# Latents scaled in the weight loop and turned ahead of the indexer; transposes over two kinds of PSUM banks; GpSimd's residual passes moved in the code

## The chip, the core and the metric

The kernel runs on one core of a Trainium2 chip. The core has TensorE (PE, matrix products; PEld is its weight load), VectorE (DVE), ScalarE (ACT) and GpSimd (POOL) for arithmetic, and SyncE (SP), whose queue issues nearly all loads here. Each engine works its own queue in order; the order within each queue is fixed when the kernel is built. The metric is the device time of one execution in microseconds (us), the median of several runs. The profile is of one execution of its own.

## The reference

All data is float32. `x` has 256 tokens of 1024 features. Block 1 (two layers of attention and MLP, with a context of 256 further tokens) comes first and is not changed by this diff but for the end of its last MLP. Block 2 has two layers, each of the form below (cut to what matters).

```python
h = x * (1 + scale) + shift                      # modulation, from a second conditioning vector
p_cq, p_ckv, p_kr, p_qb, ..., p_qi, p_ki, p_wi, p_gate = split(h @ w_in[l])
cq, ckv = rms_norm(p_cq, q_norm_g[l]), rms_norm(p_ckv, kv_norm_g[l])   # the latents: 768 and 256 features
qa, ka, va = heads(cq @ w_uq[l]), heads(ckv @ w_uk[l]), heads(ckv @ w_uv[l])
o_a = mla_attention(qa, rope part of qa, ka, rope(p_kr), va)
o_b = dilated_attention(qb, kb, vb)
score = sum_h w_idx[h] * relu(q_idx[h] . k_idx)  # the indexer
o_c = attention of each query over its top 64 keys by score
y = concat(o_a, o_b, o_c) * silu(p_gate)
x = layer_norm(4 ** 0.25 * x + (1 + gate) * (y @ w_out[l]), ln_g[l], ln_b[l])
```

The first layer's `x` is an RMS norm of block 1's result. So between block 1 and layer 0, and again between layer 0 and layer 1, the same thing has to happen: a norm over tokens, the modulation, and a transpose into feature-major form for the next products. A second copy of the normed `x`, times 4 ** 0.25 and without the modulation, is the residual that each layer's end needs.

## The kernel before

**Tiles.** The 256 tokens are two token tiles `t` of 128. Token-major tensors are [128 tokens, 1024 features]; the input of the products is feature-major, in two float32r parts, `hi` and `lo` (`ahi`, `alo`), each as two tiles of four 128-feature chunks. Every product is three matmuls (`mm3`, lines 317 to 322: hi x hi, lo x hi, hi x lo). Large tensors share one pool of 24 buffers (`k4`), small column vectors one pool of 48 (`sm`). PSUM's eight banks are four "mm", two "s", one "pt" and one "om".

**Weights.** `Weights` walks a fixed plan (class `Weights`, L169). SP loads a piece of 512 KB into one of four `raw` buffers (L184); ACT casts it to `whi` (L197); DVE subtracts to get `wlo` (L199), five buffers each, two pieces ahead of use. `W.hold` names a DVE instruction behind which all later `wlo` splits have to be issued.

**The order of the work.** The code is written as one long sequence; when the kernel is built, a planner lays each engine's queue in order from a model of durations, taking what is ready by its model, code order first.

**End of block 1 (`mlp1`).** For each token tile: the last products, gate and residual (L1227, L1228), sum of squares on ACT (L1229), the power -1/2 on POOL (L330, in `rsqrt`), then z = x * rstd * gr (L1235), z + sr (L1236), and `turn_input` for each half of the features: four transposes into the bank "pt" (L1248), `ahi` by ACT (L1250), `alo` by DVE (L1251). Each call for half 0 sets `W.hold`, so the later call, of token tile 1, is the one that the next layer's splits stand behind. Then POOL makes the residual in place, in two passes a token tile (L1239, L1240).

**`block2_layer`.** A loop over 14 weight pieces computes, for both token tiles, the two halves of the latents (key 0 and 1; L1563 multiplies by the gain row `lgain`, L1567 sums squares) and two value tensors (key 2 and 3), token tile 1 three pieces behind token tile 0. The gain's load waits, through a one-element copy on POOL (`after`, L358), for the residual of token tile 0 (`xa[0]`). Then come the indexer's inputs (`b2misc`, `b2qi`), the indexer (`sel`: per head a score step on DVE, then 16 rounds of the 8 largest and their removal, L1495 and L1496, each round with a new `sm` tile), and only then `latents(t)`: three small DVE steps, the power, the scales (L1589, L1590), four groups of transposes all in bank "pt" (L1594), copies by ACT and DVE (L1596, L1597) into `chi` and `clo`. After that the q and k products of the second attention (L1630 takes them out of PSUM), three pairs of its heads, the products from the latents, three pairs, the indexer's attention in two pairs, the gate and the output projection. `finish(t)` norms a token tile as it is done (L1737, L1740) and turns it. Behind both, with the order fixed by hand behind the second power and the last `ahi` copy, the residual for the next layer: a scaling of `lnb` (L1756), two small POOL steps a tile (L1760, L1761), ACT's scaling (L1763), and four POOL passes (L1766), tile 0 and 1 times `lng`, then tile 0 and 1 plus `lnb`.

Of the kernel before, what the change touches and what calls it, by code (L numbers as in the profile page):

```python
# [270 lines left out]
class Net:  # L271
# [897 lines left out]
    def mlp1(self, a):  # L1169
# [25 lines left out]
        for e in range(8):  # L1195
            hid[e] = [self.k4([128, 4, 256], F32R, name="hid") for _ in range(2)]
            for g in range(2):
                relu2(e, g, self.narrow("m1w1", a, "s").rearrange("p a b -> p (a b)"))
            if e == 0:

                xt = [self.k4([128, 1024], name="xt") for _ in range(2)]
                for k in range(0, 8, 4):
                    for t in range(2):
                        pt = self.psum("pt", [128, 4, 128])
                        for kk in range(4):
                            nc.tensor.transpose(pt[:, kk], hx[k + kk][:, cols(t)], self.ident)
# [12 lines left out]
        for t in range(2):  # L1219
            for i in (0, 2, 1, 3):  # L1220
                product(7, i, t, ws[i])
# [3 lines left out]
            for i in range(2):  # L1225
                c = cols(i, 512)
                V.tensor_tensor(z[:, c], acc[t][i], gate[:, c], op=OP.mult)  # L1227
                V.tensor_tensor(x[:, c], z[:, c], x[:, c], op=OP.add)  # L1228
                nc.scalar.activation(z[:, c], x[:, c], AF.Square, accum_out=ss[:, i:i + 1])  # L1229
            s1 = self.sm([128, 1])  # L1230
            V.tensor_tensor(s1, ss[:, 0:1], ss[:, 1:2], op=OP.add)
            rstd = self.rsqrt(s1, 1, 1.0 / D, 1e-6, True)
            for i in range(2):
                c = cols(i, 512)
                V.scalar_tensor_tensor(z[:, c], x[:, c], rstd, gr[:, c], op0=OP.mult, op1=OP.mult)  # L1235
                V.tensor_tensor(z[:, c], z[:, c], sr[:, c], op=OP.add)  # L1236
                self.turn_input(z[:, c], i, t, hi4, lo4)
            with self.tc.issue_after(self.pow.ins):
                nc.gpsimd.tensor_scalar(x, x, rstd, ALPHA, op0=OP.mult, op1=OP.mult)  # L1239
                nc.gpsimd.tensor_tensor(x, x, fr, op=OP.mult)  # L1240
        return [[t[:, i] for t in f for i in range(4)] for f in (hi4, lo4)], xt

    def turn_input(self, u, i, t, hi4, lo4):

        nc = self.nc
        pt = self.psum("pt", [128, 4, 128])
        for k in range(4):
            nc.tensor.transpose(pt[:, k], u[:, cols(k)], self.ident)  # L1248
        hv, lv = (f[i][:, :, cols(t)] for f in (hi4, lo4))
        self.last_hi = nc.scalar.copy(hv, pt)  # L1250
        op = nc.vector.tensor_tensor(lv, pt, hv.bitcast(F32), op=OP.subtract)  # L1251
        if i == 0:
            self.W.hold = op.ins


# [274 lines left out]
                                     start=kt == 0, stop=kt == qt)  # L1530
        nc.scalar.copy(yt, o)

    def block2_layer(self, l, a, xa):
# [13 lines left out]
        def token_step(i, t, w):  # L1547
# [13 lines left out]
            else:  # L1561
# [3 lines left out]
                for j in range(key + 1):  # L1565
                    cc = slice(256 * j, 256 * j + 512 // (key + 1))
                    nc.scalar.activation(junk[:, cc], ps[:, cc], AF.Square, accum_out=cst[t][:, key + j:key + j + 1])  # L1567

        steps = ([(g, 2 * i, 2, 512) for g in range(2) for i in range(4)] + [(2, 2 * i, 2, 384) for i in range(4)]
                 + [(3, 4 * i, 4, 256) for i in range(2)])  # L1570
        LAG, ws = 3, {}
        for i in range(len(steps) + LAG):
# [2 lines left out]
                token_step(i, 0, ws[i])  # L1575
            if i >= LAG:
                token_step(i - LAG, 1, ws.pop(i - LAG))
        chi4, clo4 = ([self.k4([128, 4, 256], F32R, name=n) for _ in range(2)] for n in ("chi", "clo"))
        chi, clo = ([t[:, i] for t in f for i in range(4)] for f in (chi4, clo4))

        def latents(t):

            s = cst[t]
            V.tensor_tensor(s[:, 0:1], s[:, 0:1], s[:, 1:2], op=OP.add)
            V.tensor_scalar(s[:, 0:1], s[:, 0:1], 256.0 / 768, None, op0=OP.mult)
            V.tensor_copy(s[:, 1:2], s[:, 2:3])
            r = self.rsqrt(s[:, 0:2], 2, 1.0 / 256, 1e-6, True)
            u = lat[t]
            V.tensor_scalar(u[:, 0:768], u[:, 0:768], r[:, 0:1], None, op0=OP.mult)  # L1589
            V.tensor_scalar(u[:, 768:1024], u[:, 768:1024], r[:, 1:2], None, op0=OP.mult)  # L1590
# [26 lines left out]
        for g in range(2):  # L1617
            nc.scalar.copy(qi[:, 2 * g:2 * g + 2], self.narrow("b2qi", a))
        sel = self.indexer(l, qi, ki, wi)
        for t in range(2):  # L1620
            latents(t)
        yt = self.feats(8, 256, name="yt")

        qb, kb = (self.k4([128, 3, 256], name="qkb") for _ in range(2))
# [127 lines left out]
                    finish(t)  # L1752
        if l == 1:
            return None, None

        nc.gpsimd.tensor_scalar(lnb, lnb, ALPHA, 0.0, op0=OP.mult, op1=OP.add)  # L1756
        for x, (mv, rstd) in zip(z, mvs):
            r2, nb = self.sm([128, 1]), self.sm([128, 1])
            with self.tc.issue_after(self.pow.ins):
                nc.gpsimd.tensor_scalar(r2, rstd, ALPHA, 0.0, op0=OP.mult, op1=OP.add)  # L1760
                nc.gpsimd.tensor_scalar(nb, mv[:, 0:1], r2, -1.0, op0=OP.mult, op1=OP.mult)  # L1761
            with self.tc.issue_after(self.last_hi.ins):
                nc.scalar.activation(x, x, AF.Identity, bias=nb, scale=r2)  # L1763
# [3 lines left out]
        return (hi, lo), z  # L1767

    def rope2(self, x, n):

# [17 lines left out]
def build(nc, tc, A, out, stop=9):  # L1788
    with tc.tile_pool(name="sb", bufs=1) as sb, tc.tile_pool(name="ps", bufs=1, space=PSUM) as ps:
# [2 lines left out]
        if stop <= 1:  # L1792
            return
        a = net.block1_l1(a)
        a, xa = net.mlp1(a)
        if stop <= 2:
            return
        for l in range(2):
            a, xa = net.block2_layer(l, a, xa)
            if stop <= 3 + l:  # L1800
                return

# [17 lines left out]
```

## Time and profile before

| What | us |
|---|---|
| Median of 3 runs (lowest to highest) | 1473.42 (1472.79 to 1475.20) |
| Profiled execution, its own time | 1476.02 |
| Its span | 1474.2 |
| PE busy | 1382.9 |
| DVE busy | 1016.8 |
| ACT busy | 639.2 |
| POOL busy | 270.7 |
| Handover 1 (end of `mlp1`, start of layer 0) | about 1027 to 1060 |
| Layer 0, latents' transposes | 1128 to 1137 |
| Handover 2 (end of layer 0, start of layer 1) | about 1249 to 1284 |
| Layer 1, latents' transposes | 1344 to 1352 |

Times in the profile count from the span's start. A timeline row shows a start, a duration, the engine, the line and the operation with what it writes and reads, how many instructions the row joins, and in brackets how long the engine was idle before it and what released it. A row that joins several instructions gives the time from the first one's start to the last one's end. In a window row each engine's busy time stands with its number of instructions; PEclk is the TensorE clock that was granted, as a share of 2.4 GHz. Busy PE is not PE at its peak, and the time between the span and the execution's own time (1.8 us) lies around the span.

### The profile page before, as it was taken

To read this page: it belongs to the slowest core of one execution; us is meant where nothing else is said; L and a number is where in the kernel's file an instruction comes from. 1 tells how busy PE (TensorE), PEld (TensorE's weight loads), DVE (VectorE), ACT (ScalarE), POOL (GpSimd) and SP (SyncE) were. 2 spreads that over 40 slices of the span, in tenths; PEclk is the share of its full clock that TensorE was granted. 3 is DMA by queue.
4 is the path that set the end of the run, shared out by engine and by line. 5 is a ranking of instruction groups with operands and counts; after the bars stand their busy time and mean duration, and the time that the engine had idled before them with its cause. 6 is when DMAs were issued, how large, how long until landed. Compare 5 with 4: busy or idle time off the path is not lost.

```text
span 1474.2 us, 23024 instructions
## 1 busy us (share of the span) xinstructions
PE 1382.9 (94%) x8779; PEld 1166.3 (79%) x8779; DVE 1016.8 (69%) x1879; ACT 639.2 (43%) x1221; POOL 270.7 (18%) x290
## 2 busy tenths in 40 slices
PE   6899999999999999999999999999796999796997
PEld 4776668988878777888989989898696788695786
DVE  4586666648977889878677664455657668666666
ACT  4355444342223222245565564444353554352552
POOL 0200011230011213441000131111200315400312
PEclk9999999999999999999999989999898999998999
DMA  9825551136578887833132266556272354473331
GB/s 320 271 72 189 172 190 40 58 115 203 177 247 272 271 300 261 275 106 118 59 100 72 86 207 204 182 179 200 81 209 85 119 192 146 132 198 105 125 123 71
DMA packets 183438, 240.79 MB, mean 163 GB/s; under 512 B 22399, under 2 KB 147360, under 8 KB 183328
## 3 DMA queue, kind: packets, MB, share of 16 engines
q1 hardware_dynamic: 172960, 235.37, 49.7%
q10 hardware_dynamic: 8576, 3.89, 1.0%
q8 instruction: 69, 1.13, 0.3%
q0 software_dynamic: 1792, 0.06, 0.1%
q14 instruction: 41, 0.34, 0.1%
HBM read 237.26 MB, written 2.03 MB: 162 GB/s over the span
## 4 chain that ended last, share of the span: by engine, by line
PE 74%; DVE 13%; DMA 4%; issue 3%; POOL 3%; ACT 2%; SPq 0%; ACTq 0%; DVEq 0%; POOLq 0%
PE mm L320 17%; PE mm L321 17%; PE mm L322 17%; PE s L321 3%; PE s L322 3%; PE s L320 3%; DVE wlo L199 2%; PE om L1074 2%; DMA adaw<-in_ada_w 2%; PE s L1512 1%; PE pt L1059 1%; PE om L1529 1%; PE mm L499 1%; PE om L1400 1%; ACT whi L197 1%
## 5 line engine op out<-in xcount | busy, mean ns | idle before, releaser
L199 DVE TENSOR_TENSOR wlo<-raw,whi 128x1024 fp32r<-128x1024 f32 (+3 forms) x282 | 355.9, 1268 | 186.3 <-ACT whi L197 176.8
L197 ACT CAST whi<-raw 128x1024 fp32r<-128x1024 f32 (+3 forms) x282 | 289.6, 1034 | 329.2 <-PE mm L321 175.9
L320 PE MATMUL mm<-ahi,whi 128*128 128x256 f32 (+1 forms) x848 | 288.1, 340 | 0.0
L321 PE MATMUL mm<-alo,whi 128*128 128x256 f32 (+1 forms) x848 | 285.0, 336 | 0.0
L322 PE MATMUL mm<-ahi,wlo 128*128 128x256 f32 (+1 forms) x848 | 284.8, 336 | 0.0
L320 PEld LDWEIGHTS mm<-ahi,whi 128*128 128x128 f32 x848 | 164.0, 193 | 20.4 <-issue 3.6
L322 PEld LDWEIGHTS mm<-ahi,wlo 128*128 128x128 f32 x848 | 163.3, 193 | 18.2 <-issue 2.4
L321 PEld LDWEIGHTS mm<-alo,whi 128*128 128x128 f32 x848 | 163.6, 193 | 16.0 <-issue 1.8
L366 POOL TENSOR_TENSOR hid<-e,hid 128x512 fp32r<-128x512 f32 x48 | 78.1, 1627 | 353.9 <-ACT hid L365 353.7
L531 DVE SCALAR_TENSOR_TENSOR acc<-adaw,cst,acc 128x1024 f32<-128x1024 f32 x98 | 128.0, 1320 | 0.5 <-DMA adaw<-in_w_ada 0.2
L320 PE MATMUL mm<-hid,whi 128*128 128x512 f32 (+1 forms) x288 | 106.7, 371 | 0.0
L321 PE MATMUL mm<-hid,whi 128*128 128x512 f32 (+1 forms) x288 | 106.0, 368 | 0.0
L322 PE MATMUL mm<-hid,wlo 128*128 128x512 f32 (+1 forms) x288 | 105.9, 368 | 0.0
L320 PE MATMUL s<-ahi,whi 128*128 128x256 f32 x256 | 73.1, 286 | 1.2 <-ACT ahi L367 1.2
L321 PE MATMUL s<-alo,whi 128*128 128x256 f32 x256 | 72.9, 286 | 0.1
L322 PE MATMUL s<-ahi,wlo 128*128 128x256 f32 x256 | 72.7, 284 | 0.0
L321 PE MATMUL mm<-wlo,ahi 128*128 128x256 f32 (+1 forms) x192 | 64.2, 335 | 6.5 <-DVE wlo L199 6.5
L320 PE MATMUL mm<-whi,ahi 128*128 128x256 f32 (+1 forms) x192 | 65.1, 340 | 2.8 <-ACT ahi L1250 2.8
L322 PE MATMUL mm<-whi,alo 128*128 128x256 f32 (+1 forms) x192 | 63.7, 333 | 0.0
L320 PEld LDWEIGHTS mm<-hid,whi 128*128 128x128 f32 x288 | 54.1, 188 | 10.2 <-issue 0.4
L322 PEld LDWEIGHTS mm<-hid,wlo 128*128 128x128 f32 x288 | 54.2, 188 | 9.7
L321 PEld LDWEIGHTS mm<-hid,whi 128*128 128x128 f32 x288 | 54.2, 188 | 9.2
(352 smaller groups left out, 2856.2 us busy)
## 6 DMA issues: line engine op xcount, KB each, us to landing
raw<-in_mlp_w SPq DMA_DIRECT2D x128, 512.0 KB, 4.2
adaw<-in_ada_w SPq DMA_DIRECT2D x96, 512.0 KB, 4.7
raw<-in_w_in SPq DMA_DIRECT2D x64, 512.0 KB, 4.0
adaw<-in_w_ada SPq DMA_DIRECT2D x48, 512.0 KB, 4.8
raw<-in_odd_w_in SPq DMA_DIRECT2D x24, 512.0 KB, 4.1
raw<-in_w_out SPq DMA_DIRECT2D x16, 512.0 KB, 5.4
raw<-in_even_w_in SPq DMA_DIRECT2D x12, 512.0 KB, 6.0
raw<-in_even_w_out SPq DMA_DIRECT2D x8, 512.0 KB, 3.5
```

The costliest lines, as they stand in the source:

```text
L197: self.nc.scalar.copy(hi[:, :m], raw)
L199: self.nc.vector.tensor_tensor(lo[:, :m], raw, hi[:, :m].bitcast(F32), op=OP.subtract)
L320: mm(ps, w[0], x[0], start=start, stop=False, skip_group_check=skip)
L321: mm(ps, w[0], x[1], start=False, stop=False, skip_group_check=skip)
L322: mm(ps, w[1], x[0], start=False, stop=stop, skip_group_check=skip)
L366: return (lo_eng or nc.vector).tensor_tensor(lo, t, hf, op=OP.subtract)
L499: nc.tensor.matmul(ps[32 * j:32 * j + 32], self.cs1[:, k, :], raw[:, 256 * j:256 * j + 256], start=k == 0, stop=k == 7)
L531: V.scalar_tensor_tensor(acc, raw, s, acc, op0=OP.mult, op1=OP.add)
L1059: nc.tensor.transpose(pt[:, kt], e[:, cols(kt)], self.ident)
L1074: nc.tensor.matmul(o[64 * hh:64 * hh + 64, cols(qt)], self.v[ab][:, 4 - nkt + i, cols(j // 2, 64)], PT[:, i, hh], start=i == 0, stop=i == ...
L1400: nc.tensor.matmul(o, PT[:, kt], self.vs[g][:, kt, cols(hh)], start=kt == 0, stop=kt == 3)
L1512: nc.tensor.matmul(s[:, c0:c0 + n], qf(h, cols(qt)), kf(h, slice(0, n)), start=True, stop=True)
```

## The change

- In `mlp1` the first transposes of `x` use the banks "pt" and "om" in turn, and `turn_input` uses "pt" for half 0 and "s" for half 1.
- In `mlp1` the squares go to a scratch tile; the product with the row `gr` is a pass of its own ahead of the power; behind it one pass does both the multiply by rstd and the add of `sr`.
- `W.hold` is set only by the first turned half of token tile 0.
- The residual is made by a function `resid(t)` that the next layer calls, in the code behind its latents; the hand-made order of those steps is gone, and in layer 0's the passes go tile by tile.
- The gain's load waits for the first turned tile (`a[0][0]`) instead of the residual.
- `latent_scale(t)` is called inside the weight loop when the token tile's second latent half is summed (piece 7); the transposes follow the loop, ahead of `b2misc` and the indexer, in banks "pt" and "om".

```diff
@@ mlp1
-                        pt = self.psum("pt", [128, 4, 128])
+                        pt = self.psum("om" if t else "pt", [128, 4, 128])
...
+        rstds = []
         for t in range(2):
             for i in (0, 2, 1, 3):
                 product(7, i, t, ws[i])
...
-                nc.scalar.activation(z[:, c], x[:, c], AF.Square, accum_out=ss[:, i:i + 1])
+                junk = self.e()
+                nc.scalar.activation(junk, x[:, c], AF.Square, accum_out=ss[:, i:i + 1])
             s1 = self.sm([128, 1])
             V.tensor_tensor(s1, ss[:, 0:1], ss[:, 1:2], op=OP.add)
             rstd = self.rsqrt(s1, 1, 1.0 / D, 1e-6, True)
             for i in range(2):
                 c = cols(i, 512)
-                V.scalar_tensor_tensor(z[:, c], x[:, c], rstd, gr[:, c], op0=OP.mult, op1=OP.mult)
-                V.tensor_tensor(z[:, c], z[:, c], sr[:, c], op=OP.add)
+                V.tensor_tensor(z[:, c], x[:, c], gr[:, c], op=OP.mult)
+            for i in range(2):
+                c = cols(i, 512)
+                V.scalar_tensor_tensor(z[:, c], z[:, c], rstd, sr[:, c], op0=OP.mult, op1=OP.add)
                 self.turn_input(z[:, c], i, t, hi4, lo4)
-            with self.tc.issue_after(self.pow.ins):
-                nc.gpsimd.tensor_scalar(x, x, rstd, ALPHA, op0=OP.mult, op1=OP.mult)
-                nc.gpsimd.tensor_tensor(x, x, fr, op=OP.mult)
-        return [[t[:, i] for t in f for i in range(4)] for f in (hi4, lo4)], xt
+            rstds.append(rstd)
+
+        def resid(t):
+            nc.gpsimd.tensor_scalar(xt[t], xt[t], rstds[t], ALPHA, op0=OP.mult, op1=OP.mult)
+            nc.gpsimd.tensor_tensor(xt[t], xt[t], fr, op=OP.mult)
+            return xt[t]
@@ turn_input
-        pt = self.psum("pt", [128, 4, 128])
+        pt = self.psum("s" if i else "pt", [128, 4, 128])
...
-        if i == 0:
+        if i + t == 0:
             self.W.hold = op.ins
@@ block2_layer
-        self.after(gain, xa[0])
+        self.after(gain, a[0][0].bitcast(F32))
...
+        def latent_scale(t):
+            s = cst[t]
+            V.tensor_tensor(s[:, 0:1], s[:, 0:1], s[:, 1:2], op=OP.add)
+            V.tensor_scalar(s[:, 1:2], s[:, 2:3], 3.0, None, op0=OP.mult)
+            r = self.rsqrt(s[:, 0:2], 2, 1.0 / 768, 1e-6, True)
+            u = lat[t]
+            V.tensor_scalar(u[:, 0:768], u[:, 0:768], r[:, 0:1], None, op0=OP.mult)
+            V.tensor_scalar(u[:, 768:1024], u[:, 768:1024], r[:, 1:2], None, op0=OP.mult)
...
                 token_step(i - LAG, 1, ws.pop(i - LAG))
+            for t in range(2):
+                if i - LAG * t == 7:
+                    latent_scale(t)
...
-        def latents(t):
...
+        for t in range(2):
             for i in range(2):
-                pt = self.psum("pt", [128, 4, 128])
+                pt = self.psum("om" if i else "pt", [128, 4, 128])
                 for k in range(4):
-                    nc.tensor.transpose(pt[:, k], u[:, 512 * i + 128 * k:512 * i + 128 * k + 128], self.ident)
+                    nc.tensor.transpose(pt[:, k], lat[t][:, 512 * i + 128 * k:512 * i + 128 * k + 128], self.ident)
...
+        xa = [resid(t) for t in range(2)]
...
         sel = self.indexer(l, qi, ki, wi)
-        for t in range(2):
-            latents(t)
@@ block2_layer, end of layer 0
-        nc.gpsimd.tensor_scalar(lnb, lnb, ALPHA, 0.0, op0=OP.mult, op1=OP.add)
-        for x, (mv, rstd) in zip(z, mvs):
-            r2, nb = self.sm([128, 1]), self.sm([128, 1])
...
-        for o, row in ((OP.mult, lng), (OP.add, lnb)):
-            for x in z:
-                nc.gpsimd.tensor_tensor(x, x, row, op=o)
+        def resid(t):
+            mv, rstd = mvs[t]
+            if t == 0:
+                nc.gpsimd.tensor_scalar(lnb, lnb, ALPHA, 0.0, op0=OP.mult, op1=OP.add)
             r2, nb = self.sm([128, 1]), self.sm([128, 1])
+            nc.gpsimd.tensor_scalar(r2, rstd, ALPHA, 0.0, op0=OP.mult, op1=OP.add)
+            nc.gpsimd.tensor_scalar(nb, mv[:, 0:1], r2, -1.0, op0=OP.mult, op1=OP.mult)
+            nc.scalar.activation(z[t], z[t], AF.Identity, bias=nb, scale=r2)
+            for o, row in ((OP.mult, lng), (OP.add, lnb)):
+                nc.gpsimd.tensor_tensor(z[t], z[t], row, op=o)
+            return z[t]
```

## Rows read from the trace of the kernel before

**Rows 1.** The page, part 1: busy us of each engine (share).

```profile
PE 1382.9 (94%) x8779; PEld 1166.3 (79%) x8779; DVE 1016.8 (69%) x1879; ACT 639.2 (43%) x1221; POOL 270.7 (18%) x290
```

**Rows 2.** Windows; the first line names the columns.

```profile
core 0: us, PE busy (x) PEld busy (x) DVE busy (x) ACT busy (x) POOL busy (x), PEclk, DMA share, GB/s
1036.00:1043.00 7.00, 5.88 (x21) 4.35 (x21) 4.18 (x8) 1.44 (x3) 4.43 (x3) 0.76 0.14 42
1043.00:1048.00 5.00, 0.43 (x4) 0.47 (x4) 3.49 (x7) 1.33 (x4) 1.55 (x2) 0.98 0.36 125
1048.00:1054.00 6.00, 4.83 (x14) 3.12 (x14) 4.96 (x5) 2.12 (x3) 3.29 (x2) 0.50 0.00 0
1054.00:1060.00 6.00, 6.00 (x19) 4.75 (x18) 3.14 (x4) 0.69 (x2) 0.00 (x0) 0.66 0.82 250
1117.65:1128.26 10.61, 0.01 (x1) 0.03 (x1) 9.79 (x31) 0.00 (x0) 0.72 (x1) 0.75 0.24 83
1128.26:1136.40 8.14, 6.28 (x29) 5.89 (x29) 3.42 (x8) 2.87 (x7) 1.00 (x3) 0.50 0.20 56
1140.76:1175.34 34.58, 33.86 (x230) 25.30 (x230) 22.58 (x62) 17.71 (x47) 11.41 (x14) 1.00 0.36 112
1252.50:1274.83 22.33, 19.23 (x85) 14.12 (x84) 16.85 (x20) 8.68 (x10) 14.19 (x10) 1.00 0.32 94
1274.83:1280.28 5.45, 0.01 (x2) 0.01 (x1) 1.88 (x3) 1.16 (x3) 1.62 (x1) 0.97 0.71 216
1280.28:1284.00 3.72, 3.72 (x10) 2.98 (x11) 2.10 (x3) 1.40 (x5) 0.00 (x0) 0.59 0.72 220
```

**Rows 3.** Timeline of VectorE, latents of layer 0: start, duration, instruction, idle before.

```profile
1071.28 0.15 DVE L1586 COPY sm<-sm 128x1 f32<-128x1 f32 x1
...
1126.45 0.15 DVE L328 TENSOR_SCALAR sm<-sm 128x2 f32<-128x2 f32 x1
...
1127.50 0.62 DVE L1589 TENSOR_SCALAR lat<-lat,sm 128x768 f32<-128x768 f32 x1 [0.44 <-POOL sm L330]
1128.03 0.35 DVE L1498 TENSOR_SCALAR sel<-score 128x384 f32<-128x384 f32 x1
```

**Rows 4.** Timeline of ScalarE, same stretch.

```profile
1132.84 1.22 ACT L1630 ACTIVATE qkb<-mm 128x256 f32<-128x256 f32 x4
```

**Rows 5.** Timeline of TensorE, first pair of layer 0.

```profile
1142.58 0.36 PE L322 MATMUL mm<-chi,wlo 128*96 128x256 f32 x1
```

**Rows 6.** Timeline of VectorE, handover 1.

```profile
1040.49 0.69 DVE L1251 TENSOR_TENSOR alo<-pt,ahi 128x512 fp32r<-128x512 f32 x1 [2.06 <-ACT ahi L1250]
...
1045.40 1.42 DVE L1235 SCALAR_TENSOR_TENSOR z<-xt,sm,rows 128x512 f32<-128x512 f32 x2 [0.68 <-POOL sm L330]
1046.73 1.29 DVE L1236 TENSOR_TENSOR z<-z,rows 128x512 f32<-128x512 f32 x2
```

**Rows 7.** Timeline of TensorE, start of the MLP.

```profile
869.09 0.66 PE L1206 MATMUL pt<-cst,hx 128*128 128x128 f32 x4 [1.33 <-ACT xt L1207]
```

**Rows 8.** Timeline of VectorE, handover 2.

```profile
1263.83 1.22 DVE L199 TENSOR_TENSOR wlo<-raw,whi 128x1024 fp32r<-128x1024 f32 x1
1265.89 2.52 DVE L199 TENSOR_TENSOR wlo<-raw,whi 128x1024 fp32r<-128x1024 f32 x1 [0.84 <-ACT whi L197]
...
1278.40 0.69 DVE L1563 TENSOR_TENSOR lat<-mm,lgain 128x512 f32<-128x512 f32 x1 [6.64 <-DMA lgain<-in_q_norm_g]
```

**Rows 9.** Timeline of the SP queue, handover 2.

```profile
1274.16 0.34 SPq L1541 DMA_DIRECT2D lgain<-in_q_norm_g  x1
```

**Rows 10.** Timeline of GpSimd: two handovers and the stretch between.

```profile
1035.99 1.89 POOL L1239 TENSOR_SCALAR xt<-xt,sm 128x1024 f32<-128x1024 f32 x1 [1.67 <-DVE z L1235]
...
1223.89 1.21 POOL L1756 TENSOR_SCALAR rows<-rows 128x1024 f32<-128x1024 f32 x1
...
1263.87 10.15 POOL L1766 TENSOR_TENSOR z<-z,rows 128x1024 f32<-128x1024 f32 x3 [3.80 <-ACT z L1763]
```

**Rows 11.** Timeline of ScalarE, handover 2.

```profile
1262.54 2.38 ACT L1763 ACTIVATE z<-z,sm 128x1024 f32<-128x1024 f32 x2
```

More of the change, by code (lines that the diff above doesn't have):

```diff
@@ L1234, in mlp1 @@
                 c = cols(i, 512)
-                V.scalar_tensor_tensor(z[:, c], x[:, c], rstd, gr[:, c], op0=OP.mult, op1=OP.mult)
-                V.tensor_tensor(z[:, c], z[:, c], sr[:, c], op=OP.add)
+                V.tensor_tensor(z[:, c], x[:, c], gr[:, c], op=OP.mult)
+            for i in range(2):
+                c = cols(i, 512)
+                V.scalar_tensor_tensor(z[:, c], z[:, c], rstd, sr[:, c], op0=OP.mult, op1=OP.add)
                 self.turn_input(z[:, c], i, t, hi4, lo4)
-            with self.tc.issue_after(self.pow.ins):
-                nc.gpsimd.tensor_scalar(x, x, rstd, ALPHA, op0=OP.mult, op1=OP.mult)
-                nc.gpsimd.tensor_tensor(x, x, fr, op=OP.mult)
-        return [[t[:, i] for t in f for i in range(4)] for f in (hi4, lo4)], xt
+            rstds.append(rstd)
[3 more added lines that the diff above has]
+            return xt[t]
+        return [[t[:, i] for t in f for i in range(4)] for f in (hi4, lo4)], resid
     def turn_input(self, u, i, t, hi4, lo4):
         nc = self.nc
-        pt = self.psum("pt", [128, 4, 128])
+        pt = self.psum("s" if i else "pt", [128, 4, 128])
         for k in range(4):
@@ L1249, in turn_input @@
         hv, lv = (f[i][:, :, cols(t)] for f in (hi4, lo4))
-        self.last_hi = nc.scalar.copy(hv, pt)
+        nc.scalar.copy(hv, pt)
         op = nc.vector.tensor_tensor(lv, pt, hv.bitcast(F32), op=OP.subtract)
-        if i == 0:
+        if i + t == 0:
             self.W.hold = op.ins
@@ L1531, in block2_pair, with block2_layer @@
         nc.scalar.copy(yt, o)
-    def block2_layer(self, l, a, xa):
+    def block2_layer(self, l, a, resid):
         nc, V, A = self.nc, self.nc.vector, self.A
@@ L1577, in block2_layer @@
                 token_step(i - LAG, 1, ws.pop(i - LAG))
+            for t in range(2):
+                if i - LAG * t == 7:
+                    latent_scale(t)
         chi4, clo4 = ([self.k4([128, 4, 256], F32R, name=n) for _ in range(2)] for n in ("chi", "clo"))
         chi, clo = ([t[:, i] for t in f for i in range(4)] for f in (chi4, clo4))
-        def latents(t):
[L1583 to L1590, printed above, removed]
+        for t in range(2):
             for i in range(2):
-                pt = self.psum("pt", [128, 4, 128])
+                pt = self.psum("om" if i else "pt", [128, 4, 128])
                 for k in range(4):
-                    nc.tensor.transpose(pt[:, k], u[:, 512 * i + 128 * k:512 * i + 128 * k + 128], self.ident)
+                    nc.tensor.transpose(pt[:, k], lat[t][:, 512 * i + 128 * k:512 * i + 128 * k + 128], self.ident)
                 hv, lv = (f[i][:, :, cols(t)] for f in (chi4, clo4))
@@ L1754, in block2_layer @@
             return None, None
-        nc.gpsimd.tensor_scalar(lnb, lnb, ALPHA, 0.0, op0=OP.mult, op1=OP.add)
-        for x, (mv, rstd) in zip(z, mvs):
+        def resid(t):
+            mv, rstd = mvs[t]
+            if t == 0:
+                nc.gpsimd.tensor_scalar(lnb, lnb, ALPHA, 0.0, op0=OP.mult, op1=OP.add)
             r2, nb = self.sm([128, 1]), self.sm([128, 1])
[L1759 to L1763, printed above, removed]
-        for o, row in ((OP.mult, lng), (OP.add, lnb)):
-            for x in z:
-                nc.gpsimd.tensor_tensor(x, x, row, op=o)
-        return (hi, lo), z
+            nc.gpsimd.tensor_scalar(r2, rstd, ALPHA, 0.0, op0=OP.mult, op1=OP.add)
[4 more added lines that the diff above has]
+            return z[t]
+        return (hi, lo), resid
     def rope2(self, x, n):
@@ L1794, in build @@
         a = net.block1_l1(a)
-        a, xa = net.mlp1(a)
+        a, resid = net.mlp1(a)
         if stop <= 2:
@@ L1798, in build @@
         for l in range(2):
-            a, xa = net.block2_layer(l, a, xa)
+            a, resid = net.block2_layer(l, a, resid)
             if stop <= 3 + l:
```

## The prediction

> **What bounds the kernel now.** I read the page first. TensorE (PE) is busy 94% of the span [rows 1], so a gain has to come from stretches in which PE stands still or has only half its clock. The second view is the table of windows around the code that changes [rows 2]. In each row I count as lost what PE was idle, plus its busy time times what the granted clock was short of 1.00; a clock of 0.50 is the 1.2 GHz level, 1.00 the 2.4 GHz level, and values between are a mix of both. There are four places.
>
> - Handover 1, MLP to layer 0 of block 2, 1036 to 1060: (1.12 + 5.88 x 0.24) + (4.57 + 0.01) + (1.17 + 4.83 x 0.50) + 6.00 x 0.34 = 12.7 us.
> - Latents of layer 0: 10.6 idle, then 1.86 idle and 6.28 busy at 0.50 (3.1 lost): 15.6 us.
> - Handover 2, layer 0 to layer 1: 3.1 idle in the first 22.33 us, 5.45 idle, then 3.72 x 0.41 = 1.5: 10.1 us.
> - Latents of layer 1: the pattern of layer 0 a second time (it stands once), 15.6 us.
>
> Together 54 us. Outside them PE is full: in the 34.58 us after the first latents it is busy 33.86, at full clock, with DVE busy 22.58. So time won ahead of such a stretch is kept.
>
> The third view, the timeline engine by engine, says what PE waited for. At the latents DVE was in the indexer's chain of maxima until 1128.03; the latents' own first step had run at 1071.28, but the next one (L328) only at 1126.45, right behind the last maximum [rows 3]. I take the reason to be the small scratch tiles ("sm"): they are handed out in code order, and the indexer takes 16 of them first. That is inferred, not shown. ScalarE (ACT) is blocked with it: four results of the q/k products leave PSUM only at 1132.84, behind the latents' copy in ACT's queue [rows 4], so PE has no bank left either.
>
> **The change part by part.** All terms are against the profiled run's own 1476.0 us (span 1474.2), which is 2.6 us above the median of 1473.4.
>
> Latents scaled in the weight loop and turned ahead of the indexer, once in each layer. The scales (0.62 us for the larger part of a token tile [rows 3]) and the power go beside PE's products. The 16 transposes stay and run at full clock. Without the stall PE needs, from 1117.65 on, only what it did between 1128.26 and 1140.76 less the half clock and the waits, so it could be at the first pair about 15.6 us sooner. But the pairs need DVE, and the indexer's chain still ends at about 1128: the latents' steps leave it (2 x about 1 us), and it starts about 2 us later, behind the transposes. So pairs start near 1128 instead of 1140.76: 13 us, PE filling in with products that need only the turned latents. Those can run ahead of the code: matmuls from `chi`, which stand behind the pairs in the code, already lie among the first pair's scores [rows 5]. I take 13 of 15.6 in each layer, bounds 10 (the chain grows by a few us) and 15.6. Late next is the indexer's DVE chain.
>
> Two kinds of banks. In handover 1 the second group of transposes no longer waits for the first to leave its bank. DVE's `alo` of it started at 1040.49, and the second token tile's chain stood behind it in DVE's queue; I expect it about 2 us sooner. The norm's order saves more: after the power, one pass (0.71) in place of two passes for both halves (1.42 and 0.65) stands before the first transpose, 1.35 us [rows 6]; the gain product added ahead of the power costs 2 x 0.65, part of it in DVE's waits. So the second tile's transposes come some 3.5 us sooner; I put 1 us on its second group, which need not wait for its bank, and 1 us on the hold. The hold on weight splits ends after the first tile, which can give PE another step of products; but each split that slips into DVE's chain costs 1.2 us. PE still waits there, so the half clock stays. I take 5.5 of 12.7; bounds 2 (three splits slip in) and 9 (PE has enough steps to bridge its 4.57 us of idle time). The same bank edit in the MLP's start removes a single wait of 1.33 us [rows 7]: I take 1, bounds 0 and 1.3.
>
> The load of the latents' gain now hangs on the first turned tile instead of the residual. Before, VectorE's `lat` stood 6.64 us at the head of its queue for this load [rows 8], and SP issued it only at 1274.16 [rows 9], after three residual passes on GpSimd (POOL) of 10.15 us together [rows 10]. SP's weight loads waited behind it too. The turned tile exists 20 us earlier, and the load takes about 4 us, so it lands before 1271.76 even if SP is held up. All 5.45 + 1.5 us go. Half a us more comes from splits that no longer run beside the passes, and nothing is late in their place but PE's own products: 7.5, bounds 5.5 and 9.
>
> The residual passes behind the latents. They are off PE's path; what they can cost is DVE's time: a split of 1.22 us took 2.52 beside a pass [rows 8]. The planner that lays the order starts what is ready: the scaling at L1756 stands behind the whole handover in the code and ran at 1223.89, 29 us before the handover began [rows 10]. So in layer 0, where nothing holds the passes back, they may run at the power as before; in layer 1 they need scratch tiles and will run near the last latent scale. I take a cost of 1.5 us for both, bounds 0 (they fall where DVE is idle) and 10 (next part).
>
> Sum: 13 + 13 + 5.5 + 1 + 7.5 - 1.5 = 38.5, so 1437.5 for the profiled run and 1435 against the median. With the terms' bounds the likeliest case spans 1427 to 1443.
>
> **The rivals.** (a) DVE becomes the limit: passes and indexer meet, and the pairs wait. Passes last 3.38 us each [rows 10]: two such in layer 0, four in layer 1, 20.3 us; at half speed DVE loses 10 of the 38.5. 1476.0 - 28.5 - 2.6 = 1445 in median terms. For it: DVE is busy 9.79 of 10.61 us in the stall. Against it: PE has products to fill with.
>
> (b) POOL holds DVE off altogether while a pass runs. All 20.3 us are lost of the 38.5: 1476.0 - 18.2 - 2.6 = 1455. Against it, the split beside the pass got about half speed. The Trainium skill, page "SBUF — State Buffer", section "Who interferes with whom", states this rule: VectorE and GpSimd share one port pair, the one that starts first holds it for its whole instruction and the other blocks fully. By that rule the 1455 would come; the trace agrees only by half, with 2.52 us.
>
> (c) The latents do not move, because something other than the scratch tiles holds them. Then 26 of the gain is missing, and the passes' cost too: 14 is left, 1459. Against it: DVE took the latents' first steps at 1071.
>
> (d) Slower: POOL works in order, and the latents' power could stand behind all residual passes. Place: DVE waits at the scale, weight splits queue behind it, PE runs dry. Price in layer 1: ACT's two scalings 2.38 [rows 11], and on POOL four passes of 3.38: 15.9; in layer 0 two passes of 1.89 and two of 3.38: 10.5. Each layer adds 3.1 for the half clock and the splits that queue behind the scale, up to four of 1.2: 7.9. In all 42.2 against a gain of 38.5: 3.7 slower, 1477. From 11.4 us a layer on (38.5 / 2 - 7.9) it eats the gain. Against it: the power stands ahead in the code, and PE's products give it time.
>
> **How the numbers follow.** Forecast 0.66 (1427 to 1443); (a) 0.18 (1440 to 1451); (b) 0.05; (c) 0.05; (d) 0.03; more than the forecast's bounds, about 1424, 0.03. The range 1425 to 1455 leaves out most of (c), (d), half of (b) and part of the last, some 0.14. A measurement tells 0.2% (3 us) from no change. Faster 0.95, the same 0.02 (the weak side of (d) and a little), slower 0.03.
>
> **What would show it.** Right: L1594's transposes lie before the indexer's maxima, with no PE idle over 3 us there; the q/k products run through; the pairs' first DVE step comes within 2 us after `sel`; no wait of `lat` for the gain's load; no granted clock near 0.50 for 8 us after the indexer. The first handover keeps an idle stretch of 3 to 4 us. Wrong: PE idle of over 5 us before the first pair (a, b), maxima or splits of twice their length beside POOL passes (b), the power behind the passes in POOL's timeline (d), or L328 still behind the maxima (c).

## The result, and the profile after

The changed kernel took 1455.57 us (median of 4 executions, 1450.91 to 1456.69) against 1473.8 of the kernel before (1472.79 to 1475.20): a ratio of 0.987, 95% interval 0.9846 to 0.9894, 18.2 us faster. Two later timings of the same file gave 1448.86 and 1451.12, with the kernel before at 1473.46 and 1473.01: ratios of 0.9836 (0.9816 to 0.9856) and 0.9846 (0.9823 to 0.987). So the gain is 18 to 25 us where 38.5 were forecast. All three timings lie above the likeliest case (1427 to 1443), and the first is 0.6 us above the range. The profiled execution below took 1450.91, its span is 1449.1.

The page, part 1, of the changed kernel (answers to [rows 1]):

```profile
PE 1382.7 (95%) x8779; PEld 1163.8 (80%) x8779; DVE 1019.9 (70%) x1875; ACT 638.9 (44%) x1221; POOL 275.4 (19%) x290
```

PE is as busy as before, to 0.2 us. The span fell by 25.1 us because PE idles less, and not because its products became shorter. The timeline of TensorE, changed kernel, shows where it still stands (line numbers moved: L1520 is the pairs' score, L1606 the latents' transposes, L1619 and L1624 the copy and the small transposes of `misc`):

```profile
1044.10 0.50 PE L321 MATMUL mm<-wlo,ahi 128*128 128x512 f32 x1 [3.37 <-DVE sm L328]
...
1123.71 1.22 PE L1520 MATMUL s<-qkb 64*128 64x256 f32 x2 [3.62 <-DVE sm L1521]
...
1289.28 0.28 PE L1624 MATMUL om<-cst,misc 8*128 8x8 f32 x2 [2.45 <-ACT misc L1619]
...
1327.17 0.48 PE L1520 MATMUL s<-qkb 64*128 64x256 f32 x1 [3.93 <-DVE sm L1521]
```

The reader should see that the 10.6 us ahead of the latents are gone from both layers, and that a new wait of 3.6 and 3.9 us stands ahead of the first pair. The windows of the changed kernel (columns as in [rows 2]) price it: the stretch before the wait, the wait, and what follows.

```profile
1068.00:1118.00 50.00, 49.37 (x396) 46.92 (x395) 37.67 (x82) 28.22 (x47) 2.52 (x5) 1.00 0.72 199
1120.10:1123.71 3.61, 0.00 (x0) 0.00 (x0) 3.48 (x12) 0.22 (x2) 0.00 (x0) 0.91 0.00 0
1123.71:1133.00 9.29, 9.29 (x31) 6.76 (x32) 4.44 (x16) 2.17 (x8) 0.60 (x1) 0.50 0.61 200
1133.00:1140.00 7.00, 7.00 (x43) 4.60 (x42) 3.84 (x18) 3.43 (x12) 1.41 (x2) 0.98 0.55 177
```

During the wait VectorE is busy 3.48 of 3.61 us. Behind it PE is busy for 9.29 us, all at a granted clock of 0.50 (1.2 GHz). Half of that, 4.6 us, is lost: more than the wait itself.

VectorE in layer 0 of the changed kernel answers to [rows 3]:

```profile
1072.89 0.17 DVE L328 TENSOR_SCALAR sm<-sm 128x2 f32<-128x2 f32 x1
1073.87 0.62 DVE L1584 TENSOR_SCALAR lat<-lat,sm 128x768 f32<-128x768 f32 x1 [0.81 <-POOL sm L330]
...
1117.64 1.04 DVE L199 TENSOR_TENSOR wlo<-raw,whi 128x864 fp32r<-128x864 f32 x1
...
1123.36 0.29 DVE L1521 CUSTOM_DVE_ANT_0 e<-s,bb 128x128 f32<-128x128 f32 x1
...
1124.18 0.36 DVE L1506 TENSOR_SCALAR sel<-score 128x384 f32<-128x384 f32 x1
```

The latents' steps run at 1072 in place of 1126, as forecast. The pairs' first step no longer waits for them, and comes at the end of the indexer's chain. The split of 864 columns is the third of four pieces of the weights for the products from `chi` (they alone have that width): it is done at 1118.68, before PE stops at 1120.10.

The second handover, windows of the changed kernel: up to the latents' scale, beside POOL's passes, the wait for `misc`, and behind it. Below them is VectorE's first use of the gain (answers to [rows 8]).

```profile
1240.00:1270.00 30.00, 29.18 (x134) 23.48 (x134) 21.65 (x32) 11.64 (x22) 2.22 (x3) 1.00 0.59 170
1270.00:1286.84 16.84, 16.13 (x123) 15.47 (x122) 13.18 (x11) 10.72 (x18) 14.42 (x9) 1.00 0.62 183
1286.84:1289.28 2.44, 0.00 (x0) 0.00 (x0) 2.44 (x2) 1.89 (x5) 0.52 (x1) 1.00 0.00 1
1289.28:1296.00 6.72, 6.72 (x39) 5.84 (x40) 6.06 (x10) 2.08 (x3) 2.37 (x2) 0.75 0.76 188
```

```profile
1250.57 0.69 DVE L1571 TENSOR_TENSOR lat<-mm,lgain 128x512 f32<-128x512 f32 x1 [0.20 <-DMA lgain<-in_q_norm_g]
```

The 6.64 us for the gain are 0.20. In their place the passes have moved into the weight loop (POOL 14.42 of 16.84 us), and PE waits for ACT at their end.

**A ledger by stage.** Each number is how much earlier, in us, the stage's first instruction starts than in the kernel before. All count from one matmul in front of the last MLP (851.07 in the kernel before), because the time up to there differs between executions by up to 5 us. The changed kernel has three profiles.

```
first instruction of          changed (3 profiles)  latents  handovers half    products no      passes own
                                                    alone    alone     rounds  first    passes  late   scratch
indexer's scores, layer 0      3.9   5.5   3.6      -0.3      6.4       5.6     5.5      5.5     3.5   -0.2
pairs' first DVE step, layer 0 17.8  19.4  17.5     13.7      6.4      23.1     4.5     19.5    17.5   12.2
handover 2, first transpose    13.4  15.6  12.4      9.7      6.2      23.7    24.6     15.4    12.8    8.9
indexer's scores, layer 1      15.9  16.8  13.4      6.1      9.6      24.7    30.3     21.9    19.3    7.8
pairs' first DVE step, layer 1 29.5  30.4  27.0     19.9      9.7      42.3    29.0     35.5    33.0   20.0
end                            24.9  25.2  21.7     14.7      9.6      42.3    47.2     29.7    18.7   16.4
```

From the indexer's first score of layer 0 to the first pair the changed kernel gains 14 us (17.8 - 3.9), just as the forecast had it (13). By the second handover only 9.5 of them are left (13.4 - 3.9); layer 1 is alike, 13.6 and then 9.0.

### The profile page after: what moved, and what is told of

Same layout as the page of the kernel before. It is cut to its first block, busy times and chain, and to the rows that moved or that the text cites. A ratio compares the mean times of both kernels' runs of the same rounds, so it can differ in the third digit from the quotient of the medians.

```text
span 1449.1 us, 23036 instructions
## 1 busy us (share of the span) xinstructions
PE 1382.7 (95%) x8779; PEld 1163.8 (80%) x8779; DVE 1019.9 (70%) x1875; ACT 638.9 (44%) x1221; POOL 275.4 (19%) x290
## 4 chain that ended last, share of the span: by engine, by line
PE 77%; DVE 11%; DMA 4%; POOL 3%; issue 3%; ACT 2%; SPq 0%; ACTq 0%; DVEq 0%; POOLq 0%
PE mm L320 18%; PE mm L322 18%; PE mm L321 18%; PE s L321 2%; PE s L322 2%; PE s L320 2%; DMA adaw<-in_ada_w 2%; PE om L1074 2%; DVE wlo L199 2%; PE s L1520 2%; PE pt L1059 1%; PE om L1537 1%; PE mm L499 1%; PE pt L1531 1%; PE om L1408 1%
## 5 line engine op out<-in xcount | busy, mean ns | idle before, releaser
L199 DVE TENSOR_TENSOR wlo<-raw,whi 128x1024 fp32r<-128x1024 f32 (+3 forms) x282 | 359.6, 1281 | 175.8 <-ACT whi L197 167.9
```

Source lines behind the costliest of these rows:

```text
L199: self.nc.vector.tensor_tensor(lo[:, :m], raw, hi[:, :m].bitcast(F32), op=OP.subtract)
```

## The experiments

Each kernel was timed beside the kernel before; "below" is the difference of the two medians.

**The changed kernel again**, with no edit.

> The changed kernel once more, with a second profile. Its four runs were 1450.9 to 1456.7 us, and the profiled one (1450.9) is the lowest; the kernel before spread over 2.4 us. If the low run is chance, the median stays near 1455 and the second profile shows a span near 1453 with the extra 4 us in one place. If the profiled run is typical, the median comes down to about 1451 and the profile shows the same stages within 1 us.

Measured: 1448.86, below both expectations. The two profiles have the same idle times ahead of the pairs and of `misc` (to 0.01 us) and end 0.3 us apart in the ledger; in between they part by up to 2.8. Where is told under the hardware below.

**The latents alone.** The kernel before with `latent_scale`, the transposes ahead of `b2misc` and their two banks:

```diff
+            for t in range(2):
+                if i - LAG * t == 7:
+                    latent_scale(t)
...
-        for t in range(2):
-            latents(t)
```

> The kernel before with the latents alone moved (scaled in the weight loop, turned ahead of the indexer over two banks); handovers and residual passes as before. Theory A (the pairs wait for the indexer's VectorE chain, so about 9.4 us a layer are won of the forecast 13): 18.7 faster, about 1455. Rival B (the residual passes beside the latents took the rest of the 13): without them 26 faster, about 1448. Rival C (the latents do not move unless the residual passes move): about 1473.

Measured: 1460.07 (0.9917, 0.9897 to 0.9936), 13.4 below. PE's idle 3.62 and 3.75 us ahead of the first pair are there too, without a GpSimd pass near. So the passes are not what made the latents worth less than 13 a layer (rival B falls). From the scores on the two layers give 10.0 and 8.6 us, which is theory A's 9.4 a layer. What is missing of its 18.7 lies ahead of the scores: in layer 1 they lose 3.6 us against the handover's start (9.7 to 6.1). The four groups of the latents' transposes now stand there, 0.35 to 0.43 us from a group's start to the next instruction: 1.5 us. A wait of 0.62 us for a split is new. And PE's work at half clock behind the wait for the gain lasts 5.48 us where it lasted 3.09 in the kernel before: 1.2 us more lost. Together these are 3.3 of the 3.6.

**The handovers alone.** The changed kernel with `latents(t)` back behind the indexer:

```diff
         sel = self.indexer(l, qi, ki, wi)
+        for t in range(2):
+            latents(t)
```

> The changed kernel with the latents back behind the indexer; the handover edits and the place of the residual passes stay. From the stages of the two profiles the handovers gave 3.6 and 2.5 us: theory A expects 1473.8 - 6 = about 1468. If the residual passes in layer 1 (12 us of GpSimd, in which a split of VectorE takes 3.3 us in place of 1.2) cost nothing that the latents would not have hidden, the 13 us of the forecast's handover terms come: about 1461. If they cost more than the handovers give: 1474 or above.

Measured: 1462.12 (0.9927, 0.991 to 0.9944), 11.3 below. That is near the 13 of the forecast's handover terms, and theory A's 6 missed: it took 3.6 and 2.5 from the changed kernel, where the latents' transposes (1.5 us) stand ahead of the scores too. The ledger has 6.4 from the first handover and 3.4 from the second. The passes cost something in the second: a split that PE needs next takes 3.11 us beside a pass (0.96 by itself), and PE waits 3.08 us for it. VectorE, then PE, this run:

```profile
1271.54 3.11 DVE L199 TENSOR_TENSOR wlo<-raw,whi 128x768 fp32r<-128x768 f32 x1
...
1274.70 0.69 PE L321 MATMUL s<-wlo,ahi 128*128 128x384 f32 x1 [3.08 <-DVE wlo L199]
```

With 13.4 for the latents alone the sum is 24.7, and the changed kernel has 24.6 beside the same runs: the two parts add up.

**Half the rounds.** The changed kernel with `for _ in range(4)` for `range(8)` in the indexer; it keeps 32 keys a query.

> The changed kernel with 4 rounds of maxima in place of 8 a token tile in the indexer (it keeps 32 keys, not 64): 6.6 us less of VectorE's chain in each layer (4 x 0.72 and 4 x 0.93). Theory A (the first pair waits for this chain): the idle 3.6 and 3.9 us of TensorE ahead of the first pair go, and with them the half clock behind (3.6 and 2.4): up to 13.5 faster than the changed kernel, about 1442. If TensorE's waits there come from something else (a bank, ScalarE), 2 us or less.

Measured: 1435.12 (0.974, 0.9721 to 0.9758), 38.3 below the kernel before and 13.7 below the changed kernel. Windows of this run, the indexer and the first pair of layer 0:

```profile
1095.00:1130.00 35.00, 34.93 (x282) 31.00 (x281) 25.91 (x77) 18.26 (x42) 1.61 (x4) 1.00 0.60 183
```

With 6.6 us less of VectorE's chain in a layer PE neither stops nor falls to half clock, and each layer gives 17.5 to 18.1 us from the scores on. This confirms theory A: the wait is for the indexer's chain.

**The products first.** The changed kernel with the q products from the turned latents (108 matmuls a layer) ahead of the first three pairs in the code; the weights keep their order, since the pairs take none. (The expectation names the k products too; the edit leaves them behind the pairs.)

```diff
+        qa = [self.k4([96, 3, 256], name="qa") for _ in range(2)]
+        ka = [self.k4([96, 3, 256], name="ka") for _ in range(2)]
+        for hh in range(2):
+            w2 = [self.W.get("b2uq") for _ in range(2)]
...
+            V.tensor_copy(ka[hh][64:96], kr.unsqueeze(1).to_broadcast([32, 3, 256]))
         for i in range(3):
             self.block2_pair((2 * i, 2 * i + 1),
...
-        qa = [self.k4([96, 3, 256], name="qa") for _ in range(2)]
...
```

> The changed kernel with the q and k products from the turned latents ahead, in the code, of the three pairs of the second attention; nothing is left out. The changed kernel is 24.6 us under the kernel before in its five rounds (1448.9). Theory A (TensorE stands 3.6 and 3.9 us and then runs at half clock because the next scores, which wait for VectorE's indexer chain, stand ahead in its queue of products that could run): 10 to 13 faster than the changed kernel, about 1437. Rival (the products' weight splits then stand in the same VectorE chain, 0.95 us each, and it ends later by as much as TensorE has more to do): within 3 us of the changed kernel.

Measured: 1427.04 (1425.78 to 1427.64; 0.9676, 0.9657 to 0.9695), 47.6 below the kernel before and 22 to 29 below the three timings of the changed kernel. Windows of this run, from the weight loop's end to the pairs of layer 0, and the same in layer 1:

```profile
1080.00:1145.00 65.00, 65.00 (x507) 57.03 (x505) 52.92 (x127) 33.63 (x66) 13.93 (x17) 1.00 0.60 178
1270.00:1345.00 75.00, 74.52 (x566) 64.00 (x565) 64.39 (x153) 38.62 (x80) 20.85 (x17) 1.00 0.53 154
```

Not a single idle us in 65, at full clock, with all the rounds done. VectorE's `sel` and its first step of the pairs, same run:

```profile
1121.97 0.35 DVE L1506 TENSOR_SCALAR sel<-score 128x384 f32<-128x384 f32 x1
...
1135.66 0.29 DVE L1521 CUSTOM_DVE_ANT_0 e<-s,bb 128x128 f32<-128x128 f32 x1
```

The pairs' first step comes 13.7 us after `sel` and 13 to 15 us later than in the changed kernel, and the end comes 22 to 25 us sooner. The indexer's chain is as long as before (26.0 us from the first score to `sel`, 25.5 in the changed kernel); PE has something to do meanwhile. The rival (the splits lengthen the chain) falls. The gain over the changed kernel is about twice the 10 to 13 expected: 9.5 us in layer 0, 8.3 in layer 1 and some 4 in the second handover, where PE no longer waits for `misc` (by the ledger, against the three profiles' mean). In layer 0 the wait and the half clock behind it, 3.6 + 4.6 us in the windows above, are most of the 9.5.

**No passes.** The changed kernel without the four row passes (`z * lng`, `z + lnb`) of the second handover, so that layer 1's residual lacks them.

> The changed kernel without GpSimd's four row passes of the second handover (the residual of layer 1 lacks its row weights). Theory B (these passes hold VectorE's splits for whole passes, 3.3 us in place of 1.2 three times, and their rows hold the buffer of a turned latent, for which ScalarE waits 4.57 us): TensorE's idle 0.7 and 2.45 us and its half clock behind, 1.7, go: 4 to 5 faster than the changed kernel, about 1444.5. If this delay is hidden behind the indexer's chain, which ends last: 1 us or less. If a pass costs more than the stretch shows: 9 or more.

Measured: 1444.67 (0.9805, 0.9783 to 0.9827), 30 below; the second handover and weight loop give 6.5 in the ledger (21.9 - 15.4) where the changed kernel has 2.5, 1.2 and 1.0. The passes cost 4 to 5.5 us there.

**The passes late.** The changed kernel with `xa = [resid(t) ...]` moved behind both sets of pairs.

> The changed kernel with the call of the residual passes behind both sets of pairs, ahead of the products of the indexer's attention; nothing is left out. If the passes cost only what they meet in the weight loop: as the run without them, 4 to 5 faster than the changed kernel. If VectorE is held wherever they run: no change, 1449. If the longer life of the rows and residuals takes buffers from the pairs: slower than the changed kernel by some us.

Measured: 1454.32 (0.9853, 0.9833 to 0.9874), no gain. The ledger has 6.5 in the second handover again, and then loses 6.2 between the indexer's attention and the end (24.8 at `qkc`, 18.7 at the end): the passes now stand among that attention's steps. They cost about as much in the one place as in the other.

**Own scratch tiles.** The kernel before with one line changed.

```diff
-                m8 = self.sm([128, 8])
+                m8 = self.sb.tile([128, 8], F32, name="m8", tag="m8", bufs=16)
```

> The kernel before with one line changed: the indexer's 16 rounds take their small results from a pool of their own, not from the common small scratch tiles. Theory of the forecast (these tiles, handed out in code order, held the latents' second step behind the maxima): the latents go ahead of the maxima by themselves, and most of what the latents alone gave (13.4) comes: about 1461. If something else held them (rival c): no change, 1473.

Measured: 1457.16 (0.9882, 0.9863 to 0.99), 17.5 below, from one line, where about 13 were expected. VectorE in layer 0 of this run (L328 stood at 1126.45 in [rows 3]):

```profile
1094.02 0.36 DVE L328 TENSOR_SCALAR sm<-sm 128x2 f32<-128x2 f32 x2
1095.01 0.65 DVE L1589 TENSOR_SCALAR lat<-lat,sm 128x768 f32<-128x768 f32 x1 [0.62 <-POOL sm L330]
```

The forecast had only inferred that the shared scratch tiles held the latents. This shows it: with tiles of their own for the maxima the latents go ahead with the code left as it was.

**Products first and own scratch tiles**, in the changed kernel:

> The changed kernel with the products from the turned latents ahead of the pairs (as in the run before, 47.6 under the kernel before) and the indexer's maxima in scratch tiles of their own. Nothing that TensorE still waits for there hangs on scratch tiles (0.5, 0.7 and 3.4 us in the first handover, 0.8 in the second): no further gain, 47 +- 2 under the kernel before. If the tiles still order VectorE's steps somewhere: 3 or more.

Measured: 1429.31 (0.9697, 0.9679 to 0.9715), 44.6 below, just under the 45 to 49 expected: no further gain. The same two edits in the kernel **before**, without anything of the change:

> The kernel before with two edits and nothing of the change: scratch tiles of their own for the maxima, and the products from the turned latents ahead, in the code, of the pairs. If the latents go ahead by themselves and TensorE has the products to run while VectorE ends the indexer: the 19 and 17 us a layer of the run with the products first, 36 under the kernel before, about 1438; the handovers' 11 stay away. If the single bank for the latents' transposes or their place behind the indexer still binds: as the run with own scratch tiles alone, 17.5, about 1457.

Measured: 1445.07 (0.9802, 0.9782 to 0.9822), 28.8 below, between the two expectations: 15.7 and 13.7 from the two layers. The latents' steps behind the indexer and the single bank still cost PE 1.64 us of idle time a layer.

**The passes in pieces.** The changed kernel with each row pass as four of 256 columns.

> The changed kernel (24.6 under the kernel before) with each of GpSimd's four row passes of the second handover cut into four of 256 columns. If GpSimd holds VectorE off for one whole instruction at a time: a split waits for a quarter pass, about 0.6 us, takes some 1.8 in place of 3.3, and most of the 4.5 us that the passes cost comes back: 2 to 4 faster than the changed kernel. If both run at half speed side by side, whatever the size: no change. If GpSimd's cost per instruction counts, the passes end later and the turned latent's buffer with them: 1 to 3 slower.

Measured: 1456.05 (0.9878, 0.9859 to 0.9897), 0.5 to 7 us above the changed kernel's three timings; in the ledger the second handover falls from +2.5, +1.2 and +1.0 to -2.5. Timeline rows of VectorE's splits, POOL's passes and ACT's copy of a turned latent, changed kernel:

```profile
1278.47 6.67 DVE L199 TENSOR_TENSOR wlo<-raw,whi 128x1024 fp32r<-128x1024 f32 x2
...
1280.66 6.70 POOL L1776 TENSOR_TENSOR z<-z,rows 128x1024 f32<-128x1024 f32 x2
...
1287.39 0.59 ACT L1608 CAST chi<-om 128x512 fp32r<-128x512 f32 x1 [4.57 <-POOL z L1776]
```

and the run with pieces:

```profile
1276.88 6.80 DVE L199 TENSOR_TENSOR wlo<-raw,whi 128x1024 fp32r<-128x1024 f32 x4
...
1289.09 0.59 ACT L1608 CAST chi<-om 128x512 fp32r<-128x512 f32 x1 [8.16 <-POOL z L1778]
...
1290.98 0.38 PE L1624 MATMUL om<-cst,misc 8*128 8x8 f32 x2 [6.04 <-ACT misc L1619]
```

A split takes 1.70 us beside pieces where it took 3.3 beside whole passes, so POOL holds VectorE for one instruction at a time. But the four passes take 15.8 us in place of 12.2 (1273.23 to 1289.06, and 1275.12 to 1287.36), and ACT's copy into `chi`, which waits for the last of them, is held 8.16 us instead of 4.57. PE's wait for ACT grows from 2.45 to 6.04. So it is this wait, and not the slow splits, that sets the passes' price here. In the run without passes the copy does not wait. Nor does it in the run with the products first, whose rows of POOL, VectorE and ACT are

```profile
1262.98 12.34 POOL L1776 TENSOR_TENSOR z<-z,rows 128x1024 f32<-128x1024 f32 x4
...
1265.11 12.43 DVE L199 TENSOR_TENSOR wlo<-raw,whi 128x832 fp32r<-128x832 f32 x5 [2.50 <-ACT whi L197]
...
1271.73 0.59 ACT L1608 CAST chi<-om 128x512 fp32r<-128x512 f32 x1
```

There the passes and the five splits are as slow as in the changed kernel (12.24 and 12.33 us), but the copy into `chi` runs while the passes do. The second handover and weight loop give 5.7 us in the ledger (30.3 - 24.6) against 6.5 without any passes: with the same slow splits and no wait of the copy, the passes cost 0.8.

**A third timing of the changed kernel.**

> The changed kernel a third time. Its two timings differ: 18.2 under the kernel before (1455.57) and 24.6 (1448.86). In the two profiles the low clock behind the same idle time lasts longer in one than in the other (in the first handover to 1051 against 1045, some 7 against 3 us of it; ahead of the first pair 9 against 7). If that is chance of each execution, the runs fall over the whole range from 1448 to 1457 and the median between 1449 and 1456, with the stages of the third profile between the other two or at one of them. If it belongs to the chip or the hour, the runs cluster at one end.

Measured: 1451.12 (1448.69 to 1453.55). The 13 executions of the three timings fill 1447.6 to 1456.7; why the first timing lies at the upper end stays open.

## Why the prediction was wrong

- **What was lost before** (54 us) was right: the run with the products first wins 47.2 of it, and from the last MLP to the output PE has one wait of over 1 us left, 3.38 in the first handover.
- **Latents, the step that failed.** "13 us, PE filling in with products that need only the turned latents. Those can run ahead of the code." The latents moved for the reason given, and the first pair was reached 14 and 13.6 us sooner. The filling did not happen. The next scores of the pair, whose bank waits for VectorE behind the last maxima, stand in PE's queue ahead of the products from `chi`, whose weights were split, three pieces of four; PE stood at the scores and did not pass them. The matmul from `chi` among the scores in [rows 5] was taken as proof that these products are free to fill in; it showed only that a few are laced between the scores. So 3.6 and 3.9 us of idle time came back, and behind each a half clock that the forecast excluded ("no granted clock near 0.50 for 8 us after the indexer"). The 13 + 13 became 9.5 + 8.6 on the mean of the three profiles: 8 us short. Put in the right order in the code, the same products made it 19 + 17.
- **Handover 1**: 5.5 + 1 forecast, 6.4 with the handovers alone, 3.6 to 5.5 in the changed kernel. PE's idle time is 3.37, in the "3 to 4" named. What PE waits for is no longer the turned tile but a weight split, which VectorE does behind the second tile's gate and residual and ends at 1044.04 (the bracket at 1044.10 names a small step beside it; in the third profile it names the split):

```profile
1042.83 1.21 DVE L199 TENSOR_TENSOR wlo<-raw,whi 128x1024 fp32r<-128x1024 f32 x1
```

- **Handover 2**: the load's wait is gone (`lat` waits 0.20 us at 1250.57 in place of 6.64, [rows 8]), as forecast. But of 7.5 - 1.5 only 1.0 to 2.5 came. The passes, priced at 1.5, cost 4 to 5.5: the 2.45 us wait for `misc` and the half clock behind it (granted 0.75, 0.52 and 0.51 over the next 6.72 us in the three profiles, 1.7 to 3.3 us lost). Another 1.5 us are the latents' transposes, which now stand ahead of layer 1's scores. What was missed is a tile: the passes read rows from the pool of large buffers, `chi` takes a buffer of that pool, and the change put the passes just ahead of `chi`. That it is the rows' buffer is inferred from the code; that the copy waits for the last pass is shown by the changed kernel, the pieces and the run without passes (4.57, 8.16 and no wait). Which buffer `chi` got with the products first is not shown.
- **Rivals.** (a), VectorE as the limit, had the place and the sign right, but through the indexer's chain alone; the passes do not meet it. (b) had the mechanism right and was given 0.05 because "the split beside the pass got about half speed". That was a misreading of [rows 8] and [rows 10]: the first of the three passes, a single row in the timeline of the kernel before, is

```profile
1263.87 3.46 POOL L1766 TENSOR_TENSOR z<-z,rows 128x1024 f32<-128x1024 f32 x1 [3.80 <-ACT z L1763]
```

and ends at 1267.33. The split of 2.52 us ends at 1268.41, 1.08 us later. It did not run at half speed: it waited for the pass's end and then ran at its own. The pass had waited in the same way: a split was running from 1263.83 to 1265.05 [rows 8], and the pass ends 2.28 us after that, about what the fourth pass takes with no split beside it:

```profile
1274.10 2.35 POOL L1766 TENSOR_TENSOR z<-z,rows 128x1024 f32<-128x1024 f32 x1
```

A split that arrives at a pass's start waits for all of it and is recorded with 3.3 us. The Trainium skill, page "SBUF — State Buffer", section "Who interferes with whom", has this rule: a VectorE instruction with two inputs in SBUF contends with a GpSimd instruction that reads SBUF, and the lock on the ports that they share is exclusive. The trace agrees in full, not by half. The price of (b), 20.3 us, was too high all the same: without layer 1's four passes 4 to 5.5 us came back, and with the products first they cost 0.8. Layer 0's passes, which run at the power as before, were not tried; one split beside them takes 2.81 us (at 1035.83). (c) and (d) fall: the latents moved, and layer 1's power ran at 1271.99, ahead of the passes from 1275.12 on.

The sum by stage: 6.5 + 13 + 6 + 13 = 38.5 forecast; 4.3 + 9.5 + 1.6 + 8.6 = 24 on the mean of the three ledgers. The ledger counts from the one profile of the kernel before, which took 1476.02, 2.2 us above the median.

## What to carry to other kernels

Idle time on an in-order engine is won only if work that is ready stands ahead of the work that waits: after a stall's cause is removed, read what is next in the queue and what it waits for, and move independent products ahead of it in the code. An instruction's stretched duration beside another engine is read by its end against the other's end, not by a ratio. A pass moved off the critical path still holds its buffers; look up which tile takes them next.

## What the hardware did that was not expected

The same idle time does not cost the same half clock. Windows of 7.5 us behind PE's 3.37 us of idle time in the first handover, in the first, second and third profile of the changed kernel:

```profile
1044.10:1051.60 7.50, 6.81 (x20) 4.91 (x21) 5.30 (x7) 2.69 (x5) 5.83 (x3) 0.54 0.53 175
```

```profile
1041.50:1049.00 7.50, 6.92 (x27) 5.00 (x28) 6.03 (x8) 2.70 (x5) 5.86 (x3) 0.77 0.53 175
```

```profile
1043.42:1050.92 7.50, 6.59 (x20) 4.71 (x21) 5.30 (x7) 2.69 (x5) 5.83 (x3) 0.55 0.53 175
```

The idle time ahead is equal to 0.01 us and PE's instructions come in the same order. In the first profile the clock fell 0.46 us behind the matmul at 1044.10 and was back at 1.00 7.3 us behind it; in the second it fell at 0.33 and was back at 3.7, in the third at 0.74 and 7.6. Ten of the profiles have this wait, of 3.37 to 3.39 us. In five the clock fell 0.25 to 0.35 us behind it and was back after 3.7 to 3.8; in the other five it fell at 0.46 to 0.74 and was back after 7.3 to 7.6. What sets the moment of the fall is not shown.

Ahead of the first pair of layer 0 the idle times are 3.62, 3.62 and 3.60, and the clocks of the 9.3 us behind are 0.50, 0.63 and 0.50. At such places the ledger's three columns part, by 0.6 to 2 us at each. The changed kernel has four of them; the kernel with the products first has one left, and its four timed executions lie within 1.9 us (1425.78 to 1427.64), where those of the changed kernel lie within 4.5 to 5.8. That these places are what spreads the executions is not shown: the passes in pieces have the same four, and those executions lie within 2.8.
